# First layer: k, q and v in three units of 512 columns, weights split by row halves in a ring of three, lower parts on POOL

## The chip, the cores and the metric

One core of one Trainium2 chip runs the whole program in one launch. Its engines are TensorE (PE; its weight loads are shown as PEld), VectorE (DVE), ScalarE (ACT), GpSimd (POOL) and the DMA queue that SyncE (SP) issues. The metric is the device time of that launch in microseconds, as the median of repeated runs; lower is better.

## What is computed

A block of two layers over 1024 tokens of 1024 features, all in float32. The change is in the first layer's mixer, whose input projection is, cut to what matters:

```
zb, zc, zh, q, k, v, qi, ki, wi = split_cols(h @ w_in, EVEN_SPLITS)   # h: 1024 x 1024; q, k, v: 512 columns each
y_a = zb * causal_dwconv(zc * zh, conv_w)
q = apply_rope(rmsnorm(heads(q), q_norm_g), cos_a, sin_a)            # 8 heads of 64
k = apply_rope(rmsnorm(heads(k), k_norm_g), cos_a, sin_a)
...
rel   = relu(einsum('bqhd,bkd->bqhk', qi, ki)); score = einsum('bqhk,bqh->bqk', rel, wi)
_, idx = top_k(where(causal, score, -inf), 256)                       # the keys that each query may see
y_b = softmax attention of q over the selected k, v
out = concatenate([y_a, y_b]) @ w_out
```

After it come a feed-forward network, a gated embedding step, and the second layer (a gated delta rule, a feed-forward network, a gated embedding step), which the change doesn't touch.

## The kernel before, in words

Every float32 product is made of three matmuls in a rounded format: an operand is split into an upper part (`hi`, a cast on ACT) and a lower part (`lo`, the difference, a subtraction on DVE), and hi·hi, hi·lo and lo·hi are summed in PSUM. `split` (L106) is that pair of instructions; `wunit` (L119) loads a weight unit of 1 MB into the two-buffer ring `wr` and splits it in two cuts of 1024 columns into the rings `wh` and `wl` of pool `W2`, with two buffers each. All weight units of the layer go through these rings: two for the index projection, then six for k, q and v, then those of z.

Stage by stage, in the order in which the program is written (`l0_proj`, L275): the index projection (L341) norms the rows, transposes them into `hT` (two halves, each an upper and a lower tile of 128 x 8 x 512), and computes the index queries and keys; `l0_index_key` (L403) finishes the keys `kiT`; then the loop over six units of 256 columns, k k q q v v. In each unit `l0_kqv` (L486) makes eight row tiles: for each 24 matmuls (8 slices of the contraction, three terms) with a 128 x 128 block of `hT` stationary and 256 columns of weights moving, two row tiles to a PSUM bank, copied by ACT into `kqvo`. For k and q, groups of four row tiles are then squared on ACT (L500), normed on DVE (L502 to L505) and rotated on POOL by four instructions that read SBUF (L511 to L514); `l0_kqT` (L523) transposes the group before on PE, copies it on ACT and writes it to DRAM for the attention by four DMAs. v is written as it is. Ahead of the units 0, 1 and 2 stand two calls each of `l0_scores` (L442), one for each block of 128 queries: 8 heads, each with matmuls (L459, L460), a relu on ACT (L462) and a multiply and add on DVE (L465, L467) that reads two SBUF tiles; and a mask (L469).

Behind the loop, `l0_z` (L536) makes the convolution branch (`psz`: 576 matmuls of 512 columns, then `pswoa`, its output product, added to x at L572), while `l0_topk` (L578) finds each query's threshold on the scores by 31 rounds of counting, on DVE (L603) and ACT (L600), and then makes the masks (L634 to L638). The attention reads k, q and v back from DRAM.

A planner puts the instructions of each engine into one order ahead of time, by the order of the program and by its own times; on the chip each engine takes its instructions in that order. Pools that are closed give their memory to later ones, whose tiles wait for the release.

Of the kernel before, what the change touches and what calls it, by code (L numbers as in the profile page):

```python
# [9 lines left out]
F32 = mybir.dt.float32  # L10
# [10 lines left out]
P = 128  # L21
# [42 lines left out]
class _K:  # L64
# [208 lines left out]
    def l0_proj(self):  # L273
        nc, A = self.nc, self.A
        v = nc.vector  # L275
        self.scp = self.pool(self.l0, "scp")
        NSC = P * sum(i + 1 for i in range(QB0, NT))
        self.sc = self.scp.tile([P, NSC], F32, name="sc")
        self.sco = {i: P * sum(j + 1 for j in range(QB0, i)) for i in range(QB0, NT)}
        self.kD = self.dr.tile([NT, DH, H, P], F32, name="kD")  # L280
        self.qD = self.dr.tile([NT, DH, H, P], F32, name="qD")
        self.vD = self.dr.tile([S, 512], F32, name="vD")
        self.hA = self.dr.tile([S, D], F32, name="hA")
        with ExitStack() as es:
            hp = self.pool(es, "l0hT")
            hT = self.hT_tiles((hp, hp), "0")
            tabp = self.pool(es, "l0tab")
            self.psum(es, "l0ps", tp=2, kq=2)
            tk = self.pool(es, "l0tk", side="right")
            with ExitStack() as e2:  # L290
                ip = self.pool(e2, "l0idx")
                kw = ip.tile([P, NT, 72], F32, name="kw")
                kiT = ip.tile([P, S], F32R, name="kiT")
                qi = [ip.tile([P, NQB, 4, DH], F32, name=f"qi{u}") for u in range(2)]
                with ExitStack() as e3:
                    self.l0_index_proj(self.pool(e3, "l0ia"), tabp, hT, kw, qi)
# [3 lines left out]
                ws = {}  # L300
# [182 lines left out]
            o = qh[:, 4 * q:4 * q + 4, :]  # L483
            self.split(o, ql[:, 4 * q:4 * q + 4, :], pv)

    def l0_kqv(self, wk, hT, u, w):  # L486
        nc, A = self.nc, self.A
        v, gp = nc.vector, nc.gpsimd
        nm = "kkqqvv"[u]
        dst = self.kD if nm == "k" else self.qD  # L490
        for tq in range(2):
            o = wk.tile([P, 4, 256], F32, tag="kqvo", bufs=3, name=f"kqvo{u}_{tq}")
            for t2 in (0, 2):
                pv = self.tp(f"pskqv{u}_{tq}_{t2}", "kq").rearrange("p (t n) -> p t n", t=2)
                for t in range(2):
                    self.mm_R(pv[:, t, :], hT, tq * 4 + t2 + t, w)
                nc.scalar.copy(o[:, t2:t2 + 2, :], pv)
            if nm != "v":
                sq = wk.tile([P, 4, 4, DH], F32, tag="kqt1", bufs=1, name=f"kqsq{u}_{tq}")
                nc.scalar.activation(sq.rearrange("p t h d -> p t (h d)"), o, AF.Square)  # L500
                ss = wk.tile([P, 16], F32, tag="kqss", bufs=2, name=f"kqss{u}_{tq}")
                v.tensor_reduce(ss.rearrange("p (t h) -> p t h", t=4), sq, axis=AX.X, op=ALU.add)  # L502
                v.tensor_scalar(ss, ss, 1.0 / DH, EPS, op0=ALU.mult, op1=ALU.add)
                rs = self.rsqrt(wk, ss, 16)
                v.tensor_tensor(o.rearrange("p t (h d) -> p (t h) d", d=DH), o.rearrange("p t (h d) -> p (t h) d", d=DH),  # L505
                                rs[:, :, None].to_broadcast([P, 16, DH]), op=ALU.mult)
                cg, sg = self.ropeg[nm]
                tb = lambda x, a, b: x[:, tq * 4:tq * 4 + 4, None, a:b].to_broadcast([P, 4, 4, b - a])
                ov = o.rearrange("p t (h d) -> p t h d", h=4)
                t1 = wk.tile([P, 4, 4, DH], F32, tag="kqt1", bufs=1, name=f"kqt1{u}_{tq}")  # L510
                gp.tensor_tensor(t1[:, :, :, 0:32], ov[:, :, :, 32:64], tb(sg, 0, 32), op=ALU.mult)  # L511
                gp.tensor_tensor(t1[:, :, :, 32:64], ov[:, :, :, 0:32], tb(sg, 32, 64), op=ALU.mult)
                gp.tensor_tensor(ov, ov, tb(cg, 0, 64), op=ALU.mult)
                gp.tensor_tensor(o, o, t1.rearrange("p t h d -> p t (h d)"), op=ALU.add)  # L514
            late, self.late = self.late, None
            if nm != "v":
                self.late = (u, tq, o, dst)
            else:
                nc.sync.dma_start(self.vD[tq * 512:(tq + 1) * 512, (u % 2) * 256:(u % 2) * 256 + 256].rearrange("(t p) n -> p t n", p=P), o)
            if late:  # L520
                self.l0_kqT(wk, *late)

    def l0_kqT(self, wk, u, tq, o, dst):  # L523

        nc = self.nc
        for c in range(2):
            p = self.tp(f"tpkq{u}_{tq}_{c}")
            for t in range(4):
                nc.tensor.transpose(p[:, t * P:(t + 1) * P], o[:, t, c * P:(c + 1) * P], self.ident)
            oT = wk.tile([P, 4, P], F32, tag="kqT", bufs=2, name=f"kqT{u}_{tq}_{c}")  # L530
            nc.scalar.copy(oT.rearrange("p t n -> p (t n)"), p)
            for a in range(2):
                nc.sync.dma_start(dst[4 * tq:4 * tq + 4, :, (u % 2) * 4 + 2 * c + a, :].rearrange("t d n -> d t n"), oT[a * DH:(a + 1) * DH])

    def l0_z(self, yp, wk, hT, topk):
        nc, A = self.nc, self.A  # L536
# [1148 lines left out]
def _layout(I):  # L1685
# [9 lines left out]
    L["w_kqv"] = _cols(np.concatenate([k, q, v], 1), 256)  # L1695
# [41 lines left out]
```

## Time and profile before

| | |
|---|---|
| time, median of 3 runs | 3010.73 us (3004.97 to 3015.27) |
| the profiled execution's own time | 3013.33 us |
| its span in the profile | 3011.6 us |
| PE, DVE, ACT, POOL busy, share of the span | 96%, 62%, 42%, 35% |
| mean granted TensorE clock | 0.981 of full speed |

The span runs from the first to the last instruction of the profile. Busy times of PE overlap, because matmuls are pipelined: the spacing of starts tells what a matmul takes. The change lies between about 45 us and 275 us of the span; the convolution branch follows up to 406 us, its output product up to 455 us, and the first logits of the attention right behind it.

### The profile page before, as it was taken

To read this page: it belongs to the slowest core of one execution; us is meant where nothing else is said; L and a number is where in the kernel's file an instruction comes from. 1 tells how busy PE (TensorE), PEld (TensorE's weight loads), DVE (VectorE), ACT (ScalarE), POOL (GpSimd) and SP (SyncE) were. 2 spreads that over 40 slices of the span, in tenths; PEclk is the share of its full clock that TensorE was granted. 3 is DMA by queue.
4 is the path that set the end of the run, shared out by engine and by line. 5 is a ranking of instruction groups with operands and counts; after the bars stand their busy time and mean duration, and the time that the engine had idled before them with its cause. 6 is when DMAs were issued, how large, how long until landed. Compare 5 with 4: busy or idle time off the path is not lost.

```text
span 3011.6 us, 47715 instructions
## 1 busy us (share of the span) xinstructions
PE 2882.0 (96%) x19211; PEld 2401.3 (80%) x19211; DVE 1868.5 (62%) x3274; ACT 1258.6 (42%) x2225; POOL 1043.4 (35%) x931
## 2 busy tenths in 40 slices
PE   7999998999999998999999999999999999989999
PEld 6989876787888886787887777788677888867877
DVE  5799995565444447984456777664455444468861
ACT  4458725454333334333445555443233333344341
POOL 1341000113444437524212443342144444456342
PEclk9999998998999998999999999999999999999999
DMA  4122165201222235533333232223621222254422
GB/s 144 50 50 92 57 190 202 91 22 53 103 104 105 105 114 190 199 105 119 104 118 102 96 110 96 90 89 120 252 77 71 105 105 105 102 201 166 138 94 91
DMA packets 119822, 340.80 MB, mean 113 GB/s; under 512 B 11696, under 2 KB 34608, under 8 KB 101936
## 3 DMA queue, kind: packets, MB, share of 16 engines
q1 hardware_dynamic: 119600, 337.74, 32.6%
q8 instruction: 151, 2.47, 0.3%
q14 instruction: 71, 0.58, 0.1%
HBM read 240.64 MB, written 97.06 MB: 112 GB/s over the span
## 4 chain that ended last, share of the span: by engine, by line
PE 81%; DVE 8%; DMA 5%; ACT 3%; issue 2%; POOL 1%; SPq 0%; DVEq 0%; ACTq 0%; POOLq 0%
PE pga L850 16%; PE pgb L850 8%; PE pda L995 7%; PE pso L1344 7%; PE psp L1113 6%; PE pdb L995 6%; PE psz L216 4%; PE pgc L850 4%; PE pskqv L227 3%; PE psow L237 3%; PE psz L1604 2%; PE y L742 2%; PE pswob L237 2%; DVE sc L467 1%; DMA sl<-gfD 1%
## 5 line engine op out<-in xcount | busy, mean ns | idle before, releaser
L995 PE MATMUL pda<-sl 128*128 128x512 f32 x1056 | 253.0, 399 | 19.3 <-ACT sl L984 7.7
L995 PEld LDWEIGHTS pda<-sl 128*128 128x128 f32 x1056 | 203.1, 193 | 65.7 <-ACT sl L984 8.6
L781 POOL TENSOR_TENSOR S<-wr_gu 128x512 f32<-128x512 f32 x44 | 67.1, 1526 | 402.9 <-DMA wr_gu<-in_w_gu_dram 353.2
L995 PE MATMUL pdb<-sl 128*128 128x512 f32 x792 | 183.1, 389 | 0.0
L109 DVE TENSOR_TENSOR w2l_gu<-S,w2h_gu 128x1024 fp32r<-128x1024 f32 x44 | 74.9, 1702 | 173.9 <-ACT w2h_gu L108 173.9
L995 PEld LDWEIGHTS pdb<-sl 128*128 128x128 f32 x792 | 148.7, 188 | 30.9
L1344 PE MATMUL pso<-hh,wl_od 128*128 128x512 f32 x384 | 156.4, 407 | 0.0
L1344 PE MATMUL pso<-hh,wh_od 128*128 128x512 f32 x384 | 155.9, 406 | 0.0
L1344 PE MATMUL pso<-hl,wh_od 128*128 128x512 f32 x384 | 155.6, 405 | 0.0
L985 DVE TENSOR_TENSOR sl<-sl 128x1536 fp32r<-128x1536 f32 (+1 forms) x56 | 110.3, 1977 | 36.6 <-ACT sl L984 36.6
L984 ACT CAST sl<-sl 128x1536 fp32r<-128x1536 f32 (+1 forms) x56 | 77.1, 1376 | 132.9 <-DMA sl<-gfD 132.7
L1362 DVE SCALAR_TENSOR_TENSOR c<-pso,odcw,c 128x509 f32<-128x509 f32 (+1 forms) x144 | 107.2, 745 | 25.8 <-ACT c L1359 24.2
L779 POOL TENSOR_TENSOR T_dn<-wr_dn 128x512 f32<-128x512 f32 x44 | 78.4, 1810 | 101.3 <-PE pgb L850 52.0
L227 PE MATMUL pskqv<-wh_kqv,hh 128*128 128x256 f32 x384 | 110.0, 287 | 0.3 <-ACT wh_kqv L108 0.3
L227 PE MATMUL pskqv<-wh_kqv,hl 128*128 128x256 f32 x384 | 109.3, 285 | 0.0
L227 PE MATMUL pskqv<-wl_kqv,hh 128*128 128x256 f32 x384 | 109.1, 285 | 0.0
L108 ACT CAST w2h_gu<-S 128x1024 fp32r<-128x1024 f32 x44 | 46.4, 1054 | 147.1 <-PE pga L850 147.1
L603 DVE TENSOR_SCALAR_CACHE_REDUCE tk_junk<-sc,tk_f 128x1024 int8<-128x1024 f32 (+5 forms) x111 | 102.6, 924 | 1.8
L1113 PE MATMUL psp<-wh_pg,hh_p 128*128 128x512 f32 x256 | 101.2, 395 | 0.0
L1113 PE MATMUL psp<-wh_pg,hl_p 128*128 128x512 f32 x256 | 100.2, 391 | 0.0
L1113 PE MATMUL psp<-wl_pg,hh_p 128*128 128x512 f32 x256 | 100.1, 391 | 0.0
L153 POOL TENSOR_SCALAR nss_f<-nss_f 128x1 f32<-128x1 f32 x16 | 3.2, 200 | 279.7 <-ACT junk_f L152 279.7
(535 smaller groups left out, 8985.2 us busy)
## 6 DMA issues: line engine op xcount, KB each, us to landing
wr_gu<-in_w_gu_dram SPq DMA_DIRECT2D x44, 1024.0 KB
sl<-gfD SPq DMA_DIRECT2D x42, 768.0 KB
gfD<-Sg SPq DMA_DIRECT2D x22, 1024.0 KB
wr_dn<-in_w_dn_dram SPq DMA_DIRECT2D x22, 1024.0 KB
wr_od<-in_w_qkv_dram SPq DMA_DIRECT2D x12, 1024.0 KB
cD<-c SPq DMA_DIRECT2D x24, 512.0 KB
gfD<-g SPq DMA_DIRECT2D x22, 512.0 KB
wr_z<-in_w_z_dram SPq DMA_DIRECT2D x10, 1024.0 KB
```

Of the source, the lines that this page charges most:

```text
L216: nc.tensor.matmul(ps[:M, f * 512:(f + 1) * 512], a[:, kc, c], b[f][:, kc, :], start=(kc == 0 and i == 0), stop=(kc == KC - 1 and i == 2))
L227: nc.tensor.matmul(out, a[:, kc, c], b[:, kc, :], start=(kc == 0 and i == 0), stop=(kc == KC - 1 and i == 2))
L237: nc.tensor.matmul(ps[:, f * 512:(f + 1) * 512], a[:, kc, tsl], b[:, f * 512:(f + 1) * 512], start=(kc == 0 and i == 0), stop=(kc == nk - ...
L603: v.tensor_scalar(jk[:, :n], sc[b], fb, 0.0, op0=op, op1=ALU.add, accum_out=c)
L779: sub = lambda o, x, y: eng.tensor_tensor(o, x, y, op=ALU.subtract)
L850: nc.tensor.matmul(bank, a[:, kc, :], b[:, kc, :], start=first and kc == 0 and m == 0, stop=kc == 3 and m == 2, skip_group_check=True)
L984: nc.scalar.copy(y, x.bitcast(F32))
L985: v.tensor_tensor(x, x.bitcast(F32), y.bitcast(F32), op=ALU.subtract)
L995: nc.tensor.matmul(ps, a[:, i, c], b[:, i, :], start=first and i == 0 and k == 0, stop=i == m - 1 and k == 2, skip_group_check=True)
L1113: nc.tensor.matmul(ps, a[:, kc, c], b, start=kc == 0 and i == 0, stop=kc == KC - 1 and i == 2)
L1344: nc.tensor.matmul(ps[:, f * 512:(f + 1) * 512], a[:, kc, :], b[f][:, kc, :], start=(kc == 0 and i == 0), stop=(kc == KC - 1 and i == 2))
L1362: nc.vector.scalar_tensor_tensor(c[:, e:(f + 1) * 512], ps[:, e - d:(f + 1) * 512 - d], cw[:, k:k + 1], c[:, e:(f + 1) * 512], op0=ALU.mul ...
```

## The change

Six units of 256 columns become three of 512 (k, q, v). The weights of a unit come as two halves of the contraction (`kh` 0 and 1, 512 rows each, 128 x 2048 in SBUF); each half is a 1 MB load into `wr` and is split by the new `l0_wkqv`: casts on ACT as before, the lower part by two POOL subtractions of 1024 columns in place of two DVE ones. The split halves go round a ring of three homes: the two buffers of `wh`/`wl` in `W2`, and one new pair (16 KB a partition) in the pool `l0kqv`. The next unit's halves are asked for at the start of a unit.

A group is now two row tiles of 512 columns (`tp`, four to a unit), each in a PSUM bank of its own. For each half `kh`, both tiles get 12 matmuls with 512 moving columns; the copies to `kqvo` come after the second half. Squares, norm and rotation work on tiles of the same size as before (128 x 1024), eight times as before. The transposed group is written by eight DMAs of 64 KB in place of four of 128 KB; v by four of 512 KB as before. The score blocks stand ahead of unit 0's groups 0 and 2, and ahead of unit 1's group 0, two at a time.

```diff
-                for u in range(6):
-                    for n in (u, u + 1):
-                        if n < 6 and n not in ws:
-                            ws[n] = self.wunit(A["w_kqv"][n], (KC, 256), f"kqv{n}")
-                    if u < 3:
-                        for i in (2 * u, 2 * u + 1):
-                            self.l0_scores(sp, kw, kiT, qi, QB0 + i)
-                    self.l0_kqv(kp, hT, u, ws[u])
+                homes = itertools.cycle(((self.W2, 2), (self.W2, 2), (kp, 1)))
+                halves = lambda u: [self.l0_wkqv(u, kh, *next(homes)) for kh in range(2)]
+                w = halves(0)
+                for u in range(3):
+                    nw = halves(u + 1) if u < 2 else None
+                    for tp in range(NT // 2):
+                        n = 4 * u + tp
+                        if n in (0, 2, 4):
+                            for i in (n, n + 1):
+                                self.l0_scores(sp, kw, kiT, qi, QB0 + i)
+                        self.l0_kqv(kp, hT, u, tp, w)
+                    w = nw
+    def l0_wkqv(self, u, kh, home, bufs):
+        raw = self.W.tile([P, 2048], F32, tag="wr", bufs=2, name=f"wr_kqv{u}{kh}")
+        nc.sync.dma_start(raw, self.A["w_kqv"][u, kh])
+        w = [home.tile([P, 2048], F32R, tag=f"w{x}", bufs=bufs, name=f"w{x}_kqv{u}{kh}") for x in "hl"]
+        for a in (slice(0, 1024), slice(1024, 2048)):
+            nc.scalar.copy(w[0][:, a], raw[:, a])
+            nc.gpsimd.tensor_tensor(w[1][:, a], raw[:, a], w[0][:, a].bitcast(F32), op=ALU.subtract)
     def l0_kqv(...):
+        pss = [self.tp(f"pskqv{u}_{tp}_{t}", "kq") for t in range(2)]
+        for kh in range(2):
+            wh, wl = w[kh]
+            for t in range(2):
+                for kc in range(4):
+                    for i, (a, b) in enumerate([(xh, wh), (xh, wl), (xl, wh)]):
+                        nc.tensor.matmul(pss[t], a[:, 4 * kh + kc, c], b[:, kc, :], start=(kh + kc + i == 0), stop=(kh == 1 and kc == 3 and i == 2))
+                if kh:
+                    nc.scalar.copy(o[:, t, :], pss[t])
...
     def l0_kqT(...):
+            for c in range(2):
+                for a in range(2):
+                    nc.sync.dma_start(dst[2 * tp:2 * tp + 2, :, 4 * q + 2 * c + a, :].rearrange("t d n -> d t n"), oT[a * DH:(a + 1) * DH, c])
```

## Rows read from the trace of the kernel before

**Rows 1.** The page's head and its part 1: the span, and the busy times of the engines with their shares of it.

```profile
span 3011.6 us, 47715 instructions
PE 2882.0 (96%) x19211; PEld 2401.3 (80%) x19211; DVE 1868.5 (62%) x3274; ACT 1258.6 (42%) x2225; POOL 1043.4 (35%) x931
```

**Rows 2.** Busy time by stretch, all engines: the stretch, its length, then PE, PEld, DVE, ACT and POOL busy us with their instructions, the granted TensorE clock, the share of DMA and GB/s.

```profile
83.60:103.20 19.60, 19.60 (x166) 19.60 (x166) 14.48 (x45) 8.08 (x12) 3.31 (x3) 1.00 0.16 55
103.20:227.00 123.80, 115.49 (x828) 107.83 (x827) 115.83 (x168) 72.19 (x121) 53.55 (x24) 0.97 0.20 52
227.00:275.40 48.40, 48.40 (x406) 48.39 (x405) 45.39 (x109) 38.04 (x74) 12.22 (x6) 1.00 0.32 99
275.40:405.80 130.40, 130.40 (x577) 107.97 (x576) 120.67 (x267) 82.55 (x151) 0.20 (x1) 1.00 0.20 65
405.80:455.60 49.80, 45.04 (x195) 35.90 (x193) 43.13 (x42) 9.23 (x9) 0.00 (x0) 1.00 0.91 269
```

**Rows 3.** The chain of work that ended last, in order of time, up to 480 us: start, length, what; one piece of the DVE work among the scores, the first of the pieces in which only PE is on the chain, and the convolution branch's products.

```profile
175.81 0.93 DVE sc L467
...
222.88 10.30 PE pskqv L227 x86
...
275.36 130.60 PE psz L216 x576
```

**Rows 4.** PE in order of time: the first and the last of 19 successive matmuls of 256 columns of k, q and v; then, of another step (L1113) with blocks of activations stationary and weights moving, the first and the last of 7 successive matmuls of 512 columns. Start, length, engine, line, out<-in.

```profile
261.75 0.28 PE L227 MATMUL pskqv<-wh_kqv,hl 128*128 128x256 f32 x1
...
263.91 0.28 PE L227 MATMUL pskqv<-wh_kqv,hl 128*128 128x256 f32 x1
...
2959.74 0.39 PE L1113 MATMUL psp<-wh_pg,hl_p 128*128 128x512 f32 x1
...
2961.10 0.39 PE L1113 MATMUL psp<-wh_pg,hl_p 128*128 128x512 f32 x1
```

**Rows 5.** DVE from 104 to 230 us, groups of one line and shape: busy us and mean ns of one, and idle time before.

```profile
L109 DVE TENSOR_TENSOR wl_kqv<-wr_kqv,wh_kqv 128x1024 fp32r<-128x1024 f32 x6 | 11.7, 1961 | 4.1 <-ACT wh_kqv L108 4.1
L467 DVE SCALAR_TENSOR_TENSOR sc<-rl,wi,sc 128x512 f32<-128x512 f32 x7 | 10.6, 1508 | 0.7 <-ACT rl L462 0.4
...
L467 DVE SCALAR_TENSOR_TENSOR sc<-rl,wi,sc 128x640 f32<-128x640 f32 x7 | 9.2, 1309 | 0.2
L467 DVE SCALAR_TENSOR_TENSOR sc<-rl,wi,sc 128x384 f32<-128x384 f32 x7 | 8.9, 1277 | 1.9 <-ACT rl L462 1.1 <-DVE sc L467 0.5
...
L469 DVE TENSOR_TENSOR sc<-sc,cf 128x128 f32<-128x128 f32 x6 | 7.8, 1304 | 0.1
...
L446 DVE TENSOR_SCALAR wi<-kw 128x8 f32<-128x8 f32 x6 | 3.1, 529 | 0.0
...
L603 DVE TENSOR_SCALAR_CACHE_REDUCE tk_junk<-sc,tk_f 128x1024 int8<-128x1024 f32 x1 | 1.3, 1278 | 0.0
```

**Rows 6.** DVE in order of time: single instructions of the same lines and shapes while POOL had nothing, and one pair while POOL rotated.

```profile
118.01 0.61 DVE L467 SCALAR_TENSOR_TENSOR sc<-rl,wi,sc 128x384 f32<-128x384 f32 x1
119.74 4.37 DVE L467 SCALAR_TENSOR_TENSOR sc<-rl,wi,sc 128x384 f32<-128x384 f32 x2 [1.11 <-ACT rl L462]
...
133.02 1.22 DVE L109 TENSOR_TENSOR wl_kqv<-wr_kqv,wh_kqv 128x1024 fp32r<-128x1024 f32 x1
...
135.97 0.75 DVE L467 SCALAR_TENSOR_TENSOR sc<-rl,wi,sc 128x512 f32<-128x512 f32 x1
...
150.86 0.28 DVE L469 TENSOR_TENSOR sc<-sc,cf 128x128 f32<-128x128 f32 x1
151.06 0.16 DVE L446 TENSOR_SCALAR wi<-kw 128x8 f32<-128x8 f32 x1
...
154.53 0.88 DVE L467 SCALAR_TENSOR_TENSOR sc<-rl,wi,sc 128x640 f32<-128x640 f32 x1
...
233.51 1.22 DVE L109 TENSOR_TENSOR wl_kqv<-wr_kqv,wh_kqv 128x1024 fp32r<-128x1024 f32 x1
```

**Rows 7.** POOL: over the whole span, the group of a later step that subtracts an upper part from weights of 1024 columns; and, in order of time, the last instruction of the rotations.

```profile
L1094 POOL TENSOR_TENSOR wl_pg<-wr_pg,wh_pg 128x1024 fp32r<-128x1024 f32 x16 | 41.8, 2650 | 13.4 <-issue 10.8 <-ACT wh_pg L1093 2.6
```

```profile
252.10 2.42 POOL L514 TENSOR_TENSOR kqvo<-kqvo,kqt 128x1024 f32<-128x1024 f32 x1
```

**Rows 8.** The first units' weights: ACT's casts in order of time, and PE's matmuls of k, q and v alone (busy us, count, clock, DMA) between 46 and 54.9 us; in the 28.7 us after that there are three more.

```profile
44.93 1.99 ACT L108 CAST wh_kqv<-wr_kqv 128x1024 fp32r<-128x1024 f32 x2 [0.57 <-PE psi L227]
...
83.61 2.00 ACT L108 CAST wh_kqv<-wr_kqv 128x1024 fp32r<-128x1024 f32 x2 [10.17 <-PE psi L227]
```

```profile
46.00:54.90 8.90, 6.70 (x38) 0.81 0.37 120
```

**Rows 9.** PE in order of time after a wait of 2.80 us: matmuls of 512 columns, the first of them and one 2.7 us later.

```profile
203.16 0.79 PE L460 MATMUL pss<-kiT,qil 128*128 128x512 f32 x1 [2.80 <-DVE qil L109]
...
205.89 0.63 PE L460 MATMUL pss<-kiT,qil 128*128 128x512 f32 x1
206.31 0.63 PE L459 MATMUL pss<-kiT,qih 128*128 128x512 f32 x1
```

**Rows 10.** DVE at the end of the projection stage, in order of time: the last mask and the last sum of the convolution branch.

```profile
450.20 0.69 DVE L638 TENSOR_SCALAR sc<-tk_pf 128x1024 f32<-128x1024 f32 x1
...
454.52 1.23 DVE L572 TENSOR_TENSOR xt<-pswoa,xt 128x1024 f32<-128x1024 f32 x1 [2.49 <-PE pswoa L237]
```

**Rows 11.** The writes of the transposed k and q, issued by SP: least, median and most ns to issue one, and when.

```profile
L533 SPq DMA_DIRECT2D kD<-kqT x16: 574/608/1375, 135.1 to 209.6; - x16
```

More of the change, by code (lines that the diff above doesn't have):

```diff
@@ L299, in l0_proj @@
                 sp, kp = self.pool(e2, "l0sc"), self.pool(e2, "l0kqv")
-                ws = {}
+                homes = itertools.cycle(((self.W2, 2), (self.W2, 2), (kp, 1)))
+                halves = lambda u: [self.l0_wkqv(u, kh, *next(homes)) for kh in range(2)]
+                w = halves(0)
                 self.late = None
-                for u in range(6):
-                    for n in (u, u + 1):
-                        if n < 6 and n not in ws:
-                            ws[n] = self.wunit(A["w_kqv"][n], (KC, 256), f"kqv{n}")
-                    if u < 3:
-                        for i in (2 * u, 2 * u + 1):
-                            self.l0_scores(sp, kw, kiT, qi, QB0 + i)
-                    self.l0_kqv(kp, hT, u, ws[u])
+                for u in range(3):
[7 more added lines that the diff above has]
+                    w = nw
             with ExitStack() as e2:
@@ L484, in dupT @@
             self.split(o, ql[:, 4 * q:4 * q + 4, :], pv)
-    def l0_kqv(self, wk, hT, u, w):
+    def l0_wkqv(self, u, kh, home, bufs):
+        nc = self.nc
+        raw = self.W.tile([P, 2048], F32, tag="wr", bufs=2, name=f"wr_kqv{u}{kh}")
[4 more added lines that the diff above has]
+            nc.gpsimd.tensor_tensor(w[1][:, a], raw[:, a], w[0][:, a].bitcast(F32), op=ALU.subtract)
+        return [x.rearrange("p (k n) -> p k n", k=4) for x in w]
@@ L487, in l0_kqv @@
+    def l0_kqv(self, wk, hT, u, tp, w):
         nc, A = self.nc, self.A
         v, gp = nc.vector, nc.gpsimd
-        nm = "kkqqvv"[u]
+        nm = "kqv"[u]
         dst = self.kD if nm == "k" else self.qD
[L491 to L494, printed above, removed]
-                for t in range(2):
[L496 to L533, printed above, removed]
+        o = wk.tile([P, 2, 512], F32, tag="kqvo", bufs=3, name=f"kqvo{u}_{tp}")
@@ new lines, in l0_kqv @@
+        pss = [self.tp(f"pskqv{u}_{tp}_{t}", "kq") for t in range(2)]
+        for kh in range(2):
+            wh, wl = w[kh]
+            for t in range(2):
+                xh, xl = [x[(2 * tp + t) // 4] for x in hT]
+                c = slice((2 * tp + t) % 4 * P, ((2 * tp + t) % 4 + 1) * P)
+                for kc in range(4):
[3 more added lines that the diff above has]
+                    nc.scalar.copy(o[:, t, :], pss[t])
@@ new lines, in l0_kqv @@
+        if nm != "v":
+            sq = wk.tile([P, 2, H, DH], F32, tag="kqt1", bufs=1, name=f"kqsq{u}_{tp}")
+            nc.scalar.activation(sq.rearrange("p t h d -> p t (h d)"), o, AF.Square)
+            ss = wk.tile([P, 16], F32, tag="kqss", bufs=2, name=f"kqss{u}_{tp}")
+            v.tensor_reduce(ss.rearrange("p (t h) -> p t h", t=2), sq, axis=AX.X, op=ALU.add)
+            v.tensor_scalar(ss, ss, 1.0 / DH, EPS, op0=ALU.mult, op1=ALU.add)
+            rs = self.rsqrt(wk, ss, 16)
+            oh = o.rearrange("p t (h d) -> p (t h) d", d=DH)
+            v.tensor_tensor(oh, oh, rs[:, :, None].to_broadcast([P, 16, DH]), op=ALU.mult)
+            cg, sg = self.ropeg[nm]
+            tb = lambda x, a, b: x[:, 2 * tp:2 * tp + 2, None, a:b].to_broadcast([P, 2, H, b - a])
+            ov = o.rearrange("p t (h d) -> p t h d", h=H)
+            t1 = wk.tile([P, 2, H, DH], F32, tag="kqt1", bufs=1, name=f"kqt1{u}_{tp}")
+            gp.tensor_tensor(t1[:, :, :, 0:32], ov[:, :, :, 32:64], tb(sg, 0, 32), op=ALU.mult)
+            gp.tensor_tensor(t1[:, :, :, 32:64], ov[:, :, :, 0:32], tb(sg, 32, 64), op=ALU.mult)
+            gp.tensor_tensor(ov, ov, tb(cg, 0, 64), op=ALU.mult)
+            gp.tensor_tensor(o, o, t1.rearrange("p t h d -> p t (h d)"), op=ALU.add)
@@ new lines, in l0_kqv, with l0_kqT @@
+        late, self.late = self.late, None
+        if nm != "v":
+            self.late = (u, tp, o, dst)
+        else:
+            nc.sync.dma_start(self.vD[tp * 256:(tp + 1) * 256, :].rearrange("(t p) n -> p t n", p=P), o)
+        if late:
+            self.l0_kqT(wk, *late)
+    def l0_kqT(self, wk, u, tp, o, dst):
+        nc = self.nc
+        for q in range(2):
+            p = self.tp(f"tpkq{u}_{tp}_{q}")
+            for c in range(2):
+                for t in range(2):
+                    nc.tensor.transpose(p[:, (2 * c + t) * P:(2 * c + t + 1) * P], o[:, t, (2 * q + c) * P:(2 * q + c + 1) * P], self.ident)
+            oT = wk.tile([P, 2, 2, P], F32, tag="kqT", bufs=2, name=f"kqT{u}_{tp}_{q}")
+            nc.scalar.copy(oT.rearrange("p c t n -> p (c t n)"), p)
+            for c in range(2):
+                for a in range(2):
+                    nc.sync.dma_start(dst[2 * tp:2 * tp + 2, :, 4 * q + 2 * c + a, :].rearrange("t d n -> d t n"), oT[a * DH:(a + 1) * DH, c])
@@ L1694, in _layout @@
     L["w_kw"] = _cols(np.concatenate([ki, wi], 1), 72)[0]
-    L["w_kqv"] = _cols(np.concatenate([k, q, v], 1), 256)
+    L["w_kqv"] = np.stack([x.reshape(2, 4, P, 512).transpose(0, 2, 1, 3).reshape(2, P, 2048) for x in (k, q, v)])
     L["w_z"] = _cols(np.concatenate([x[:, j * P:(j + 1) * P] for j in range(4) for x in (zc, zh, zb)], 1), 256)
```

## Prediction

> **What bounds the kernel now.** I read the engines' shares first: PE is busy for 96% of the span, the next engine for 62% [rows 1]. So a microsecond taken off PE counts wherever PE alone is on the chain, and the question is where that is. Then I cut the stage of the change into stretches [rows 2] and laid the chain beside them [rows 3]. From 103 to 227 us DVE is busy for 115.8 of 123.8 us and the chain runs through its score sums: this stretch ends when DVE is done, and PE waits for it now and then. From 227 us on PE has no gap: the rest of k, q and v up to 275.4, then 130.4 us of the convolution branch. In that time DVE runs the top-k rounds at over nine tenths. Both meet at the end of the stage: the last mask on DVE is written at 450.9 us, the last sum of the branch, which waited 2.49 us for PE, at 455.7 [rows 10]. So the stage has two chains of nearly one length, PE's later by some 5 us, and DVE's starts when the scores are done. A gain on PE above some 5 us shows only if DVE ends earlier too; a loss on either shows in full.
>
> **Fewer, wider matmuls.** Before: 1152 matmuls of 256 columns, which start every (263.91 - 261.75)/18 = 0.120 us [rows 4], 138.2 us. After: 576 of 512 columns. The nearest row with activations stationary and weights moving has them every (2961.10 - 2959.74)/6 = 0.2267 us [rows 4]; the 576 of the branch in 130.6 us [rows 3] are as fast. 576 x 0.2267 = 130.6 us. PE: -7.7 us. The listed 0.28 and 0.39 us of one matmul overlap, and their ratio would promise far too much.
>
> **The lower parts leave DVE.** Six of the twelve subtractions lie in the stretch that DVE bounds, with 1.22 us each when POOL is still [rows 5, 6], so 7.3 us; two more come at 233 to 237 us, in the top-k [rows 6], 2.4 us. The first four are early, where DVE has room.
>
> **They arrive on POOL.** The very operation is in the trace: an upper part subtracted from weights of 1024 columns takes 2.65 us there [rows 7]; POOL's undisturbed 1024-column instruction takes 2.42, the lower bound. POOL has the time: 53.6 of 123.8 us [rows 2]. But it isn't free for DVE. While POOL rotates, two score sums of 0.61 us take 4.37 us [rows 6]. Over the stretch the groups that POOL held up cost more than their undisturbed price: sums of 384, 512 and 640 columns 8.9 - 4.3, 10.6 - 5.3 and 9.2 - 6.2; masks 7.8 - 1.7; the head weights 3.1 - 1.0; the subtractions themselves 11.7 - 7.3 [rows 5, 6]. That is 25.6 us lost beside 53.6 us of POOL, 0.48 us for each. The counts aren't slowed: 1.28 us for 1024 columns [rows 5]. A subtraction on POOL then takes 0.48 x 2.65 = 1.27 us from DVE, where it saves 1.22. Bounds: nothing, if it falls beside counts and reads of PSUM; 2.65, if DVE waits for all of it. I take the 1.27, since the rotations from which it comes stand in the same stretch among the same work. With six there as before: 6 x 0.05 = +0.3 us. In the top-k, whose work is mostly the counts, the two are gained: -2.4. DVE's chain: -2.1 us.
>
> On the same point the Trainium skill (SBUF — State Buffer, Who interferes with whom) says that a DVE instruction with two SBUF inputs and a POOL instruction that reads SBUF exclude each other for the whole instruction. The sums' rows agree in kind, with 0.48 for their size; by the rule alone the price would be the upper bound, which is the second rival below. Its Perfetto Trace Analysis (Optimizing Scalar/DVE Operations) warns that moving work between the two might not help.
>
> **The start.** Both buffers of the weight ring hold the index weights at first: k's first weights came in at 44.93 us, the second at 83.61, each as soon as PE had let a buffer go [rows 8]. Before, the first were all rows of 256 columns, enough for whole tiles: 38 matmuls, 4.6 us, fill PE's early gaps, and at 83.6 PE goes on without a break [rows 8, 2]. After, they are half the rows of 512. They serve 24 matmuls, 24 x 0.2267 = 5.4 us, as much fill, and there both PSUM banks are taken. At 83.6 nothing can go on before the other half is there: a cast of 1.0 us, then a subtraction of 2.65. The first matmul of the half needs only the cast, the second the lower part: PE waits until 87.3, 3.6 us, then has 6 matmuls, and waits 1.3 us for the second lower part. With 2.42 us each it is 3.4 and 1.1. I take 4.7 us. Bounds: nothing, if other work or a later gap takes it up; 7.7, if the clock falls as well: after a wait of 2.80 us in the scores the granted clock was at its lower level from 203 to 209 us, with 512 columns every 0.42 us [rows 9], 3 us lost.
>
> **Covered edits.** The next unit's halves have homes one by one. The pair in the new buffers can come at any time; each of the others waits until the last group of the unit before has done its first half, and then 24 + 24 matmuls, 10.9 us, cover the cast and both subtractions, 1.0 + 2 x 2.65 = 6.3 us. I cost this at nothing; if a rotation stands ahead of it in POOL's order it costs, see below. On ACT, the scores' relus are queued behind a cast that waits for its home; they did that before too. Casts, copies, squares, rotations and transposes keep number and size. SP issues 32 more writes of 0.6 us [rows 11], 19 us over more than 100 us in which it carries little; behind them only the branch's first weights are queued, and these wait for a free buffer anyway. Later stages aren't touched, though the planner makes the order anew.
>
> **The sum.** PE: -7.7 + 4.7 = -3.0 us. DVE: -2.1. The later of the ends, PE's, moves by 3.0, and DVE's mask, 5 us earlier, stays ahead of it. The profiled execution took 3013.3 us (span 3011.6 and 1.7 around it): 3010.3. It stands 2.6 us above the median of 3010.7, so on the runs' scale 3007.7, rounded to 3008. Without the start's wait it is 3003, with a fallen clock 3011; some microseconds of a new order make its own range 3002 to 3014.
>
> **Rival 1: DVE gets all that it gives.** If the planner's order puts the subtractions beside counts, copies and PSUM reads, DVE saves 7.3 + 2.4 = 9.7 us, and the start's wait is made good in the scores, where PE waits anyway; the slow stretch at 203 us may go too. Then both chains end 8 to 11 us earlier: about 3001. For it: there are only 12 subtractions in all, and DVE has over 7 us of idle time. Against it: 0.48 is the mean of seven rotations that nobody placed badly.
>
> **Rival 2, slower: POOL holds DVE for the whole of each.** Place: units q and v, whose eight subtractions fall among the scores (two of them more than before, if the units run early). Price: 8 x 2.65 - 7.3 - 2.4 = +11.5 us; with six there, +6.2. The scores' end moves, and PE and the top-k with it: 3017 to 3022, middle 3020. It decides from the point where more than 1.22/2.65 = 0.46 of a POOL subtraction is lost to DVE; the mean of the stretch, 0.48, lies right at it. For it: an isolated POOL instruction in a dense row of sums holds up the next sum at once. Against it: counts, reductions and PSUM reads lie between.
>
> **Rival 3, the seams of the ring.** If a rotation (about 7.3 us: two instructions of 2.42 and two of half their size) stands in front of the subtractions on POOL, the half is ready after 13.6 us against 10.9 of cover: 2.7 us at each of two seams, and up to 3 us each for the clock. With the sum above: 3008 + 2 x 5.7 = 3019; with waits alone, 3013. For it: POOL takes its work in order, and the rotation of a unit's third group comes due in just these microseconds. Against it: a planner that knows both would put the subtractions first, and at the first seam score products fill PE.
>
> **How the numbers follow.** Forecast 0.50, rival 1 0.20, rival 2 0.17, rival 3 0.13. A measurement of this kernel can tell about 0.3% from no change, 9 us: faster is below 3001.7, slower above 3019.8. Faster: 0.12 of rival 1 and 0.08 of the forecast's edge, 0.20. Slower: 0.10 of rival 2, 0.06 of rival 3, 0.02 of the forecast, 0.18. The range takes in the forecast and most of each rival: 2999 to 3021.
>
> **What would show it.** Right: 576 matmuls 0.227 us apart; PE waiting 4 to 5 us near 84 us for a lower part; the last score sum within 2 us of before; the branch's first matmul some 3 us earlier. Wrong: score sums with a mean well above those of before and the scores' end later by over 4 us (rival 2); PE waiting for a lower part at a change of unit (rival 3); the scores' end 7 us earlier (rival 1). It would also be wrong if the new order moved later stages by more than this one.

## The result and the profile after

The changed kernel takes 3036.69 us (median of 4 runs, 3036.22 to 3039.44); the kernel before, on the same chip, 3013.0. The ratio is 1.0082 (95% interval 1.0055 to 1.0108): by the ratio 25 us slower, outside the range of 2999 to 3021 us. The profiled execution has a span of 3034.7 us against 3011.6 [rows 1]. PE is busy for longer although it has 576 matmuls less. The page's head and part 1, after:

```profile
span 3034.7 us, 46608 instructions
PE 2888.4 (95%) x18635; PEld 2378.9 (78%) x18635; DVE 1878.9 (62%) x3262; ACT 1256.4 (41%) x2225; POOL 1071.9 (35%) x943
```

Lines have moved: casts L496, subtractions L497, matmuls L515, copies L517, rotation L531 to L534, score matmuls L462 and L463, relu L465, score sum L470, mask L472.

**Where the time went.** The same first three stretches as in [rows 2], after, all engines (length; PE, PEld, DVE, ACT, POOL busy; granted clock; DMA share; GB/s), and two of 20 us inside the second:

```profile
83.60:103.20 19.60, 15.47 (x66) 12.42 (x66) 17.19 (x25) 7.43 (x10) 9.66 (x4) 0.91 0.32 108
103.20:227.00 123.80, 106.38 (x497) 87.79 (x496) 101.03 (x160) 61.54 (x107) 58.35 (x28) 0.92 0.11 30
227.00:275.40 48.40, 46.66 (x216) 38.11 (x215) 41.25 (x76) 30.56 (x52) 22.79 (x10) 1.00 0.35 98
```

```profile
140.00:160.00 20.00, 14.71 (x59) 11.84 (x60) 18.79 (x22) 8.52 (x17) 12.31 (x6) 0.74 0.43 131
160.00:180.00 20.00, 13.79 (x63) 11.12 (x61) 18.16 (x28) 8.76 (x17) 7.80 (x4) 0.83 0.00 1
```

PE had 0.0, 8.3 and 0.0 us without work in the three stretches before [rows 2]; it has 4.1, 17.4 and 1.7 now, at a lower clock. As a rough measure of work done, take busy time by granted clock: before 19.60 x 1.00 + 115.49 x 0.97 + 48.40 x 1.00 = 180.0 us at full speed, after 15.47 x 0.91 + 106.38 x 0.92 + 46.66 = 158.6. So 21.4 us of PE's work are late by 275 us, and 3.4 of the early fill (3.00 us of k, q and v between 46 and 54.9 us at a clock of 0.69, against 6.70 at 0.81 [rows 8]). Less the 7.7 us that the wider matmuls save, that is 17 us. A count of the matmuls that start before 83.6 and before 275.4 us, each at its spacing, gives 21.7, 3.6 and 17.6. The chain of waits, after, shows the convolution branch:

```profile
299.12 124.96 PE psz L216 x551
```

It ends at 424.1; before at 275.36 + 130.60 = 406.0 [rows 3]: 18.1 us later. So the account of this branch closes to a microsecond: 18 us are lost between 46 and 275 us, by PE's waits and the clock that fell with them, and are carried from there. The spans are 23.1 us apart; the other 5 come behind the branch's 576 matmuls and aren't accounted for. The scores' last mask is 21.6 us later (247.4 against 225.8). I use one mark below, the start of the attention's last instruction that reads the logits on DVE (group by tile: least, median and most ns, first and last start), before and after:

```profile
L719 DVE CUSTOM_DVE_ANT_0 L<-psl,sc x48: 547/887/1225, 488.7 to 670.3; 128x384 f32<-128x384 f32 x8, 128x512 f32<-128x512 f32 x8, 128x640 f32<-128x640 f32 x8, 128x768 f32<-128x768 f32 x8
```

```profile
L741 DVE CUSTOM_DVE_ANT_0 L<-psl,sc x48: 505/886/1225, 508.3 to 691.0; 128x384 f32<-128x384 f32 x8, 128x512 f32<-128x512 f32 x8, 128x640 f32<-128x640 f32 x8, 128x768 f32<-128x768 f32 x8
```

It moves by 20.7 us; a second profile of the unedited changed kernel (e11) has it at 692.1. What follows the mark, which no edit touches (on DVE at most 11 of its 2277 instructions start in another order), took 2333.7 to 2347.8 us in the twenty profiles of this study, so the mark is a finer measure of the edits than one span; the runs' ratio remains the verdict. The two can differ: where that later stretch is longer, the clock mostly stood longer at its lower level in it, by the trace's clock records 70.2 us in e15 (2333.7 us long), 78.5 before (2341.3) and 94.3 in e2 (2346.4). Why isn't shown.

**What POOL does to DVE.** POOL in order of time, after: the two subtractions of k's first half; the two of k's second half and the two of q's first, almost without a gap; and later the two of q's second half with the first of v's:

```profile
45.53 5.09 POOL L497 TENSOR_TENSOR wl_kqv<-wr_kqv,wh_kqv 128x1024 fp32r<-128x1024 f32 x2 [5.14 <-ACT wh_kqv L496]
...
85.84 4.97 POOL L497 TENSOR_TENSOR wl_kqv<-wr_kqv,wh_kqv 128x1024 fp32r<-128x1024 f32 x2 [35.22 <-ACT wh_kqv L496]
91.23 4.69 POOL L497 TENSOR_TENSOR wl_kqv<-wr_kqv,wh_kqv 128x1024 fp32r<-128x1024 f32 x2 [0.42 <-issue]
...
134.93 7.04 POOL L497 TENSOR_TENSOR wl_kqv<-wr_kqv,wh_kqv 128x1024 fp32r<-128x1024 f32 x3 [4.30 <-ACT wh_kqv L496]
```

DVE beside the rows from 85.84 on:

```profile
86.04 2.50 DVE L369 TENSOR_TENSOR qi<-qi,ir 128x256 f32<-128x256 f32 x1
88.46 2.64 DVE L370 TENSOR_TENSOR qi<-qi,ir 128x256 f32<-128x256 f32 x1
91.02 0.67 DVE L413 TENSOR_REDUCE mu<-kw 128x8 f32<-128x512 f32 x1
91.73 1.93 DVE L414 TENSOR_SCALAR mu<-mu 128x8 f32<-128x8 f32 x1
93.69 2.78 DVE L417 TENSOR_TENSOR kin<-kw,mu 128x512 f32<-128x512 f32 x1
...
134.68 0.17 DVE L138 TENSOR_TENSOR rsq_a<-rsq_y 128x16 f32<-128x16 f32 x1
134.89 0.18 DVE L139 SCALAR_TENSOR_TENSOR rsq_a<-rsq_a,kqss 128x16 f32<-128x16 f32 x1
135.10 2.28 DVE L140 SCALAR_TENSOR_TENSOR rsq_y<-rsq_a,rsq_y 128x16 f32<-128x16 f32 x1
137.41 2.28 DVE L138 TENSOR_TENSOR rsq_a<-rsq_y 128x16 f32<-128x16 f32 x1
139.73 2.27 DVE L139 SCALAR_TENSOR_TENSOR rsq_a<-rsq_a,kqss 128x16 f32<-128x16 f32 x1
142.03 0.18 DVE L140 SCALAR_TENSOR_TENSOR rsq_y<-rsq_a,rsq_y 128x16 f32<-128x16 f32 x1
...
144.95 1.28 DVE L109 TENSOR_TENSOR qil<-tpd_qi,qih 128x512 fp32r<-128x512 f32 x2
```

An instruction on 16 columns, 0.17 us when POOL is still, takes 2.28 us: one DVE instruction passes for each POOL subtraction, however little it does. A reduction to 8 columns (L413) isn't held; here it starts in a gap of POOL, but in e8 (below), where it runs beside a subtraction from start to end, it takes no longer. POOL, then DVE in order of time, e8:

```profile
85.68 5.45 POOL L497 TENSOR_TENSOR wl_kqv<-wr_kqv,wh_kqv 128x1024 fp32r<-128x1024 f32 x2 [44.83 <-ACT wh_kqv L496]
...
86.45 0.68 DVE L413 TENSOR_REDUCE mu<-kw 128x8 f32<-128x512 f32 x1
```

And things stand behind the held ones. At 86 us it is the index keys' chain; ACT in order of time:

```profile
96.57 0.63 ACT L419 ACTIVATE kisq<-kin 128x512 f32<-128x512 f32 x1 [7.48 <-DVE kin L417]
97.10 1.05 ACT L517 COPY kqvo<-pskqv 128x512 f32<-128x512 f32 x2
```

ACT's copies of k's first group are queued behind a square that waits 7.48 us for DVE, and PE waits for the copies to give back its two banks. At 135 us it is the norm of k, and behind it on DVE the lower part of the index queries (`qil`, L109) that PE needs for the next scores. At 46 us it was the lower part of the transposed rows (`hl`), behind two DVE instructions held for 2.60 and 2.42 us; the poorer early fill comes with that. PE in order of time, the first matmul behind each wait:

```profile
51.63 1.12 PE L193 MATMUL tp_n<-cf,hn_n 128*128 128x128 f32 x4 [3.49 <-DVE hl L109]
...
97.72 0.80 PE L515 MATMUL pskqv<-wh_kqv,hh 128*128 128x512 f32 x1 [4.13 <-ACT kqvo L517]
...
145.69 0.79 PE L463 MATMUL pss<-kiT,qil 128*128 128x512 f32 x1 [5.29 <-DVE qil L109]
```

Around and behind the last the granted clock is 0.74 and 0.83 (windows of 20 us above). The Trainium skill (SBUF — State Buffer, Who interferes with whom) states the hold for the whole instruction, also for a DVE instruction of the fast two-port kind; these rows agree, 2.28 us beside subtractions with a median of 2.47.

### The profile page after: what moved, and what is told of

It reads as the page before. It is cut to its first block, busy times and chain, and to the rows that moved or that the text cites. A ratio compares the mean times of both kernels' runs of the same rounds, so it can differ in the third digit from the quotient of the medians.

```text
span 3034.7 us, 46608 instructions
## 1 busy us (share of the span) xinstructions
PE 2888.4 (95%) x18635; PEld 2378.9 (78%) x18635; DVE 1878.9 (62%) x3262; ACT 1256.4 (41%) x2225; POOL 1071.9 (35%) x943
## 4 chain that ended last, share of the span: by engine, by line
PE 81%; DVE 9%; DMA 3%; ACT 3%; issue 3%; POOL 1%; SPq 0%; DVEq 0%; ACTq 0%; POOLq 0%
PE pga L872 16%; PE pgb L872 8%; PE pso L1366 7%; PE pda L1017 7%; PE psp L1135 6%; PE pdb L1017 5%; PE psz L216 4%; PE pgc L872 4%; PE pskqv L515 4%; PE psow L237 3%; PE psz L1626 2%; PE y L764 2%; PE pswob L237 2%; DMA dupk<-kD 1%; PE psi L227 1%
## 5 line engine op out<-in xcount | busy, mean ns | idle before, releaser
L109 DVE TENSOR_TENSOR w2l_gu<-S,w2h_gu 128x1024 fp32r<-128x1024 f32 x44 | 73.7, 1675 | 174.5 <-ACT w2h_gu L108 174.5
L622 ACT ACTIVATE tk_junka<-sc,tk_f 128x512 int8<-128x512 f32 (+2 forms) x93 | 83.8, 901 | 40.8 <-DVE tk_f L640 29.1
L764 PE MATMUL y<-vv,pT 128*128 128x64 f32 x576 | 82.2, 283 | 6.2 <-ACT pT L758 6.2
L109 DVE TENSOR_TENSOR sl<-T_dn,sl 128x512 fp32r<-128x512 f32 x88 | 85.3, 1019 | 4.4 <-ACT sl L108 4.4
```

Of the source, the lines that this page charges most:

```text
L109: self.nc.vector.tensor_tensor(lo, src, hi.bitcast(F32), op=ALU.subtract).ins)
L764: nc.tensor.matmul(y[:, h * DH:(h + 1) * DH], pT[:, kb, :], vv[:, kb, h * DH:(h + 1) * DH], start=kb == 0, stop=kb == i)
```

## The experiments

"us" is (ratio - 1) x 3011; the expectations use differences of medians, which differ from it by up to 2 us. "Mark" is the shift of the attention's last logits in the one profile, against 670.3.

| run | kernel | ratio [95%] | us | mark |
|---|---|---|---|---|
| e11 | changed, unedited | 1.0083 [1.0069, 1.0096] | +25 | +21.8 |
| e1 | changed, all lower parts on DVE | 1.0049 [1.0030, 1.0068] | +15 | +6.1 |
| e13 | changed, k's four on POOL, q's and v's on DVE | 1.0037 [1.0025, 1.0050] | +11 | +13.0 |
| e8 | changed, k's four on DVE, q's and v's on POOL | 1.0039 [1.0024, 1.0054] | +12 | +16.3 |
| e16 | changed, one of each two on POOL | 1.0049 [1.0036, 1.0063] | +15 | +13.0 |
| e3 | loops exchanged, all on POOL | 1.0099 [1.0083, 1.0114] | +30 | +23.5 |
| e14 | exchanged, q's and v's eight on POOL | 1.0075 [1.0060, 1.0091] | +23 | +16.9 |
| e10 | exchanged, k's four on POOL | 1.0036 [1.0023, 1.0048] | +11 | +5.5 |
| e4 | exchanged, all on DVE | 1.0026 [1.0017, 1.0035] | +8 | +4.2 |
| e2 | before, all lower parts on POOL | 1.0039 [1.0026, 1.0052] | +12 | +2.5 |
| e15 | changed, POOL's subtractions cut in two | 1.0040 [1.0025, 1.0055] | +12 | +13.2 |
| e18 | as e14, cut in two | 1.0064 [1.0051, 1.0077] | +19 | +15.0 |
| e17 | as e2, cut in two | 1.0011 [1.0001, 1.0021] | +3 | +0.5 |
| e6, e5, e7 | e4 with home, with `kqT` of 3, with both | 1.0027, 1.0027, 1.0021 | +8, +8, +6 | +8.9, +8.6, +3.7 |
| e9 | e7, scores ahead of k's groups 0, 1, 2 | 1.0030 [1.0018, 1.0041] | +9 | +5.4 |
| e12 | before, only v 512 wide | 1.0007 [0.9998, 1.0015] | +2 | -4.3 |

### Which part: lower parts, or the new loops (e1 to e4)

The theory was rival 2's: POOL holds DVE. Its rival: a group that takes both PSUM banks. e1 and e2 put the lower parts on the other engine in either kernel:

```diff
-            nc.gpsimd.tensor_tensor(w[1][:, a], raw[:, a], w[0][:, a].bitcast(F32), op=ALU.subtract)
+            nc.vector.tensor_tensor(w[1][:, a], raw[:, a], w[0][:, a].bitcast(F32), op=ALU.subtract)
```

> The changed kernel with the lower parts of k, q and v subtracted on DVE again (all twelve), everything else as changed. Theory P (POOL's subtractions hold DVE up in the scores, and with them the top-k and the stage): the stage comes back, the last score sum near 230 us instead of 247, total within 6 us of the kernel before. Rival S (the new structure costs it: both PSUM banks taken by one group, so PE waits for ACT's copies, and the ring's start): the last score sum stays beyond 240 us and the total 15 us or more above the kernel before.

> The kernel before with one edit: the twelve lower parts of k, q and v are subtracted on POOL; six units of 256 columns as before. Theory P: 12 to 23 us slower than the kernel before, the tiny DVE instructions beside each subtraction 2.3 us long. Rival S: within 6 us of the kernel before.

e3 exchanges the loops, so that one bank is filled and copied at a time; e4 is e3 and e1 together:

```diff
-        for kh in range(2):
-            wh, wl = w[kh]
-            for t in range(2):
+        for t in range(2):
+            for kh in range(2):
+                wh, wl = w[kh]
```

> The changed kernel with the two loops exchanged: each row tile does both halves of the contraction before the next tile starts, so that one PSUM bank is copied while the other is filled. Theory P: the total stays within 6 us of the changed kernel. Rival S: PE's waits for ACT's copies to kqvo (13 us in the changed kernel) shrink to a few us and the total falls by 8 us or more.

> Both edits of the two runs before: lower parts on DVE and the loops exchanged. Theory P: as with DVE alone, within 4 us of that run. Rival S: at least 8 us below the run with DVE alone. If both costs are real and their sum is the whole loss, the total is at or a few us below the kernel before.

POOL costs 10 us by the runs with the loops as changed (25 to 15; 15 by the mark), 22 when exchanged (30 to 8; 19 by the mark) and 12 in the kernel before (2.5 by the mark). That it does harm in the changed kernel is shown; in e1, with the subtractions on DVE, the waits at 51.63 and 97.72 are gone. In e2 the scores' last mask is even 3.6 us earlier than before (222.2 against 225.8), and most of its 12 us lie behind the mark, so e2 doesn't show this path. Moving a subtraction also lets the planner make another order; what part of these differences is order was not separated. ACT in order of time, e1:

```profile
88.65 0.59 ACT L517 COPY kqvo<-pskqv 128x512 f32<-128x512 f32 x1 [2.77 <-PE pskqv L515]
...
90.26 0.64 ACT L419 ACTIVATE kisq<-kin 128x512 f32<-128x512 f32 x1
```

The square is ready at 90.26 instead of 96.57, and the copy goes ahead of it. The two banks cost 7 us where DVE has the lower parts (15 to 8, intervals that overlap; 1.9 by the mark); with POOL the exchange brings nothing (e3), since the copies then wait for ACT's queue and not for a bank: e3 has the same wait, 4.12 us. (The 13 us in e3's expectation add the records of PE and of its weight loads, 5.9 + 7.2, for the same waits.) e1's and e4's results lie between the two theories: e1 is 15 us slower, as rival S said, but its last score sum is at 234.1 us, and e4 is 7 us below e1. Without POOL and with one bank the change is still 8 us slower.

### Which of POOL's subtractions (e8, e10, e13, e14, e16)

```diff
-            nc.gpsimd.tensor_tensor(w[1][:, a], ...)
+            (nc.gpsimd if u else nc.vector).tensor_tensor(w[1][:, a], ...)        # e8, and e14 with the loops exchanged
+            (nc.vector if u else nc.gpsimd).tensor_tensor(w[1][:, a], ...)        # e13, and e10 with the loops exchanged
+            (nc.vector if a.start else nc.gpsimd).tensor_tensor(w[1][:, a], ...)  # e16
```

> The changed kernel with only k's four lower parts on DVE; the eight of q and v stay on POOL. If POOL's cost comes from the early four, which stand beside the index keys (their DVE instructions took 2 to 2.8 us there in place of 0.2 to 0.7), the scores start 3 us or more earlier and the total falls by 8 us or more. If it comes from those beside the scores, the scores start earlier but the total stays within 5 us of the changed kernel.

> The version with the loops exchanged, k's four lower parts on POOL and the eight of q and v on DVE. With all twelve on DVE it was 7 us above the kernel before. If the early four are what POOL costs, this one is 15 us or more above the kernel before; if the cost needs those beside the scores, it stays within 10.

> The changed kernel itself, unedited, beside the others: 20 to 28 us above the kernel before.

> The changed kernel with k's four lower parts on POOL and the eight of q and v on DVE, loops as changed. Measured so far against the kernel before: all twelve on POOL +27 to 28 us, none +14, q's and v's eight alone +12. Theory T (each part costs for itself, and the costs add): the eight cost nothing here, so the early four must cost what all cost: 28 - 12 + 14 = +30 us. Theory S (POOL's subtractions cost only where k's and q's follow one another in a row; either part alone is absorbed): +12 to +16 us.

> The changed kernel with the loops exchanged (one PSUM bank at a time), k's four lower parts on DVE, the eight of q and v on POOL. Measured so far with the loops exchanged: all twelve on POOL +30 us, none +7, k's four alone +11. Theory T (the costs add): 30 - 11 + 7 = +26 us. Theory S (they cost only together): +7 to +13 us.

> The changed kernel with one of the two lower parts of every half on POOL, the other on DVE: six subtractions on POOL, spread over all three units. Theory P (price by POOL's time): half of the 13 us, so +20 to +21 us. Theory S (only rows of subtractions on POOL cost): no row is left, +12 to +16 us.

With the loops exchanged the parts add: 8, +3 for k's four, +15 for the eight, 30 together; theory T's +26 came as +23. As the change has its loops they don't add by the runs: either part alone gives 11 or 12, no more than the 15 of none, and both together 25; theory S said that. The mark there goes by T: 6.1, 13.0, 16.3, 21. So neither theory holds in both, and with intervals of 4 us to either side I leave the split open. In three of these four comparisons (two orders of the loops, runs and mark) the eight of q and v are the dearer part. They aren't all among the scores: in the changed kernel q's first two stand beside the index keys, at 91.23 us, and v's last two start at 242.88 us, so the wait at 97.72 isn't k's alone. Half as many on POOL (e16) give 10 of the 25 us back, which is theory S's range and more than theory P's half of the price.

### The length of POOL's instructions (e15, e17, e18)

If one DVE instruction passes for each on POOL, shorter ones must hold less:

```diff
-            nc.gpsimd.tensor_tensor(w[1][:, a], raw[:, a], ...)
+            for b in (slice(a.start, a.start + 512), slice(a.start + 512, a.stop)):
+                nc.gpsimd.tensor_tensor(w[1][:, b], raw[:, b], ...)
```

> The changed kernel with each POOL subtraction of 1024 columns cut into two of 512, 24 in all, so POOL's time is the same or a little more. If one DVE instruction passes for each POOL instruction, however short it is (theory H), twice as many DVE instructions pass in the same time, and a short one is held for some 1.2 us instead of 2.28: about half of POOL's price of 13 us comes back, +20 to +22 us. If the price goes by POOL's whole time (theory P, 0.48 us or more for each us), it stays at +27 us or more.

> The kernel before, with its twelve lower parts of k, q and v on POOL as 24 subtractions of 512 columns. With twelve of 1024 on POOL it took +11 us. Theory H (one DVE instruction passes for each POOL instruction; half the length holds a short one for half as long): +3 to +7 us. Theory P (the price goes by POOL's whole time): +11 us or more. If what the pieces gave in the changed kernel was another planned order only (theory L), anything between 0 and +15 us.

> The changed kernel with the loops exchanged, k's four lower parts on DVE, q's and v's eight on POOL as sixteen of 512 columns. As eight of 1024 they took +23 us, on DVE +7. Theory H: half of the 16 us come back, +13 to +17 us, or more of them, as in the last run. Theory P: +23 us or more.

All three came down: by 13 us, 8 us, and 3 us (this one within its intervals); by the mark by 7.5, 2.0 and 1.9. POOL, then DVE in order of time, e15, eight subtractions of 512 columns:

```profile
127.93 10.52 POOL L498 TENSOR_TENSOR wl_kqv<-wr_kqv,wh_kqv 128x512 fp32r<-128x512 f32 x8
...
133.58 1.24 DVE L136 TENSOR_SCALAR rsq_y<-kqss 128x16 int32<-128x16 int32 x1
134.85 1.19 DVE L138 TENSOR_TENSOR rsq_a<-rsq_y 128x16 f32<-128x16 f32 x1
136.07 1.19 DVE L139 SCALAR_TENSOR_TENSOR rsq_a<-rsq_a,kqss 128x16 f32<-128x16 f32 x1
137.29 1.18 DVE L140 SCALAR_TENSOR_TENSOR rsq_y<-rsq_a,rsq_y 128x16 f32<-128x16 f32 x1
138.51 0.17 DVE L138 TENSOR_TENSOR rsq_a<-rsq_y 128x16 f32<-128x16 f32 x1
```

The short ones are held for 1.2 us instead of 2.28: theory H, shown in the rows, and theory P (price by POOL's time, which rose) falls with e15 and e17. The size lies in H's range in e17 alone, at its lower end (8 of 12 us came back, 2.0 of them at the mark); e15 gave back more than H said, e18 less. Theory L, another planned order, isn't excluded by the times. e18's row of short DVE instructions is long enough to meet all eight pieces: PE's waits for `qih`, a relu and `qil` in its 12 us come to 3.55 + 1.79 + 4.02 us, beside 7.87 + 1.31 in e14.

### What is left without POOL (e5 to e7, e9, e12)

e6 puts the third home of the ring into a pool that is opened earlier, as the second of the cycle; e5 gives `kqT` three buffers; e7 has both; e9 moves the scores ahead of k's groups:

```diff
-                homes = itertools.cycle(((self.W2, 2), (self.W2, 2), (kp, 1)))
+                homes = itertools.cycle(((self.W2, 2), (wp, 1), (self.W2, 2)))    # e6, e7, e9
...
-            oT = wk.tile([P, 2, 2, P], F32, tag="kqT", bufs=2
+            oT = wk.tile([P, 2, 2, P], F32, tag="kqT", bufs=3                     # e5, e7, e9
...
-                        if n in (0, 2, 4):
-                            for i in (n, n + 1):
+                        if n in (0, 1, 2):                                        # e9
+                            for i in (2 * n, 2 * n + 1):
```

> The same version (DVE, loops exchanged), with three buffers in place of two for the transposed groups, whose copies on ACT waited 4 us for the doubled number of writes. Theory W (these waits of ACT hold the relus of the scores up): ACT's waits for the writes vanish and the total falls by 3 us or more. Rival O: the total stays within 2.5 us.

> The version with the lower parts on DVE and the loops exchanged, and one edit more: the ring's third home is in a pool of its own, opened with the rotation tables, and comes second, so that both halves of k's weights can be split before 84 us. Theory H (what is left of the loss, some 7 us above the kernel before with 7.7 us of matmul time gained, is the start: k cannot go on until its second half has come and the scores start 3 us late): the scores start at 117 us or earlier, and the total falls by 4 us or more. Rival O (the waits among the scores, from order and clock, cost it): the total falls by less than 3 us.

> Both edits of the two runs before together, on the version with DVE and the loops exchanged. If theories H and W are both right, the total is below the kernel before by up to 4 us; if neither is, it stays 5 us or more above it.

> The version with DVE, loops exchanged, own home and three buffers, some 5 us above the kernel before, with the score blocks ahead of k's groups 0, 1 and 2 instead of 0, 2 and q's 0. Theory O (score products queued on PE behind lumps of k and q make DVE wait): the scores end 5 us earlier and the total falls by 3 us or more. Otherwise it stays within 3 us or rises, because k's work then comes later.

None of them moves the time by more than its interval. In e6 the scores do start at 117.0 us, as theory H asked, and the total doesn't fall; in e9 theory O's 3 us don't come. So neither the homes, nor the transposes' buffers, nor the place of the scores is by itself the cause of the 8 us; a part of 2 or 3 us can't be told from the scatter. e12 leaves k and q of the kernel before as they are and makes v alone in the new way, behind the scores, with its lower parts on DVE:

```diff
-                for u in range(6):
+                for u in range(4):
...
+                    if u == 3:
+                        vw = [self.l0_wv(kh, home) for kh, home in ((0, self.W2), (1, kp))]
...
+                for tp in range(NT // 2):
+                    self.l0_v(kp, hT, tp, vw)   # per row tile: both halves into one PSUM bank
```

> The kernel before with only v changed: one unit of 512 columns in two halves, after the scores, lower parts on DVE, one bank copied while the other is filled; k and q as before. 192 matmuls of 512 columns in place of 384 of 256 save 2.6 us of PE where PE alone is the chain. If the wide matmuls are worth what they save and only the stage of the scores spoils it: 1 to 5 us below the kernel before. If they cost anywhere: at or above it.

The 2.6 us that wider matmuls of v should save aren't seen in the runs (+2, interval -0.6 to +4.5), though the mark is 4.3 us earlier.

Where e4 loses is in its windows, the first three stretches:

```profile
83.60:103.20 19.60, 19.60 (x87) 16.22 (x88) 17.96 (x41) 4.90 (x8) 6.29 (x4) 1.00 0.30 108
103.20:227.00 123.80, 110.14 (x513) 89.71 (x512) 98.78 (x164) 69.36 (x118) 44.08 (x21) 0.93 0.15 39
227.00:275.40 48.40, 47.70 (x215) 38.58 (x214) 43.27 (x92) 33.25 (x61) 16.44 (x8) 1.00 0.33 99
```

By the same measure as above 19.60 + 110.14 x 0.93 + 47.70 = 169.7 us of PE's work, 10.3 less than before. The early fill is no loss here: 27 matmuls of 512 columns start before 83.6 us, 27 x 0.2267 = 6.1 us, against 40 of 256 before, 4.8 us. With the 7.7 us saved e4 is 9.0 us ahead at 83.6; its branch ends at 410.6 against 406.0, 4.6 us behind. So 13.6 us are lost in between, of which the rough measure sees 10.3. So the gain of the wider matmuls is there and is given back among the scores. PE's waits there, from 110 to 250 us (who, for whom, us in total, times, longest), before and in e4:

```profile
PE pss L459 <- ACT rl L462: 3.4, 5, 1.0
```

```profile
PE pss L462 <- ACT rl L465: 9.3, 8, 2.1
```

PE waits for relus, that is for a score bank, nearly three times as long. Why the relus come later in the new order wasn't settled. No version here beats the kernel before.

## Why the prediction was wrong, by its own steps

- **Fewer, wider matmuls: right.** PE in order of time, after, ten matmuls of the k unit from the first to the last: (92.07 - 90.03)/9 = 0.2267 us, as predicted. The 7.7 us are in the account of PE's work.

```profile
90.03 0.39 PE L515 MATMUL pskqv<-wh_kqv,hl 128*128 128x512 f32 x1
...
92.07 0.39 PE L515 MATMUL pskqv<-wh_kqv,hl 128*128 128x512 f32 x1
```

- **They arrive on POOL: the step that failed.** One subtraction was given 2.65 us, in fact 2.47; that was right. "0.48 us for each" us of POOL was a mean over rotations that fell beside long sums, and it priced the wrong thing: DVE's busy time. As such it held: from 44 to 275.4 us DVE's instructions took 49.6 us more than the same ones take undisturbed, beside 95.9 us of POOL, 0.52 for each; before, 35.8 beside 69.1, also 0.52. DVE's time in the second stretch even fell (101.0 us, from 115.8 [rows 2]), because it stood idle and its work moved back. The step gave DVE's chain -2.1 us and PE's none; measured, the subtractions on POOL cost 10 us by the runs and 15 by the mark (e11 against e1). The price lies in who waits for the instruction that is held: PE 3.49, 4.13 and 5.29 us. "The first four are early, where DVE has room" failed in the same way: DVE had room there, but the index keys' chain, ACT's copies and PE's banks hung on single short instructions of it.
- **The start: right in size by luck, by another path.** PE is without work for 4.1 us between 83.6 and 103.2, where 4.7 was said. But it never waited more than 0.2 us for a lower part: it waited for ACT's copies, which waited for DVE, which POOL held. The lower clock comes on top, as in the upper bound of 7.7, and so does the poorer fill, which the prediction had at "as much fill", 24 matmuls: 9 start before 83.6 us. With the subtractions on DVE it is 25 (e1) and 27 (e4).
- **Covered edits: one uncovered.** The ring's seams cost nothing to see: no wait of PE for a lower part at a change of unit, so rival 3 falls. The group that takes both banks was not priced at all; it costs 2 to 7 us (e1 against e4). What else is lost among the scores, 13.6 us of PE's work in e4, the prediction had at "some microseconds of a new order".
- **Rival 2, slower**, had mechanism and direction right: POOL holds DVE for the whole of each. Its place was right in part: four of q's and v's eight stand among the scores (134.93 and 147.33 us), the others beside the index keys and behind. Of its two signs one came: the scores end over 20 us later, but the 42 score sums take DVE 53.7 us against 54.2; the held ones are others. Its 3017 to 3022 was too low, since it added the holds to DVE's busy time and left out PE's waits behind them and the clock that falls after a wait, as it had after one of 2.80 us [rows 9].

## What to carry to other kernels

Work that goes to POOL is to be priced by the short DVE instructions that will stand beside it and by what is queued behind those on DVE, ACT and PE, not by a share of DVE's time; if it must go there, in short pieces, which cost less in all three pairs here, in one of them within its interval. Where two engines' chains end together, as here, a microsecond saved on one can be given back in gaps among the finer work beside it: work done (busy time by granted clock), stretch by stretch, shows where.

## What the runs showed of the hardware

- A DVE instruction of 16 columns takes 0.17 us alone and 2.28 us beside a POOL subtraction of 1024 columns, 1.2 beside one of 512: its time is POOL's, and one passes for each. Instructions with one tensor input of 8 or 16 columns (L414, L136) are held as well; a reduction (L413, 0.67 us; 0.68 wholly beside a subtraction in e8) is not.
- In the two windows of 20 us around and behind PE's wait of 5.29 us the granted clock was 0.74 and 0.83 on the mean of its two levels (1.2 and 2.4 GHz); before, the whole stretch had 0.97 [rows 2]. Of the 21.4 us of PE's work that are late, 15.0 are time without work (23.3 against 8.3 us), the other 6.4 the lower clock.
- Cutting POOL's subtractions costs POOL itself: 24 of 512 columns took 36.2 us in e17, twelve of 1024 31.4 in e2, and still the kernel was 8 us faster.
